# A two-layer transformer kernel: compressed values in one product of 79 rows, later steps of the compression chains, and an earlier transpose of x

## The chip, the cores and the metric

The kernel runs on one core of a Trainium2 chip. The time is device microseconds of one execution, from the first to the last thing that the core does. Three runs of the kernel before gave 2173.02, 2168.36 and 2178.68 us; the median is 2173.02. The profile is of a further execution, and its times are counted from the start of its span.

The engines are named as the profile names them: PE is TensorE (matmuls and transposes), PEld its weight loads, DVE is VectorE, ACT is ScalarE, POOL is GpSimd, and SP issues most DMA transfers.

## The reference

256 tokens of width 2048 go through two layers, all in float32. Layer 0 is an attention by stick breaking and a feed-forward part, layer 1 the native sparse attention (NSA) and a feed-forward part. The change touches the first products of layer 0 and the NSA. Of the NSA, cut to what matters:

```python
# 16 heads of 128 in 4 groups; n_cmp = (256 - 32) // 16 + 1 = 15 compressed blocks
def compress_blocks(x, pe, w1, w2):            # x: (B, G, T, 128)
    idx = arange(n_cmp)[:, None] * 16 + arange(32)[None, :]
    flat = (x[:, :, idx] + pe).reshape(B, G, n_cmp, 32 * 128)
    return gelu(flat @ w1) @ w2

kc_blk = rms_norm(compress_blocks(kc, pe[0], w1[0], w2[0]), k_norm_g[0])
vc_blk = compress_blocks(vc, pe[1], w1[1], w2[1])
p_cmp  = softmax(where(mask_c, q @ kc_blk.T * scale - slope * dist_c, NEG_INF)) * mask_c
o_cmp  = p_cmp @ vc_blk                        # 15 rows deep
o      = gates[0] * o_cmp + gates[1] * o_slc + gates[2] * o_win
```

With 256 tokens all four selection blocks are always taken, so selected and window attention are both dense causal attentions over 256 keys.

## The kernel before, in words

**Precision by split.** A float32 operand is split into a high part, rounded to the matmul's own format (F32R), and a low part, the remainder. ScalarE writes the high part (a Copy into an F32R tile) and VectorE the low part (a subtraction). Each product is then three matmuls: high by high, high by low, low by high. `split` (line 131) does it for weights, `split_evac` (line 313) for results in PSUM.

**Projections.** Weights come in raw tiles of 2 x 128 x 512 (five buffers, 512 KB each) and are split into `whi` and `wlo` tiles (four buffers each). `chunk_N` (line 153) and `chunk_T` (line 192) do the 12 or 24 matmuls of one such chunk. Between their high and their low part, and again behind them, they call `pump()`.

**Work beside the projections.** Attention, compression and the like are generators in the list `beside` (lines 101 to 121). Each `pump()` serves only the first in the list: it adds rate/2 to that generator's account and takes a step for each whole unit; a `yield 1` ends the pump's turn. `drain()` runs all that is left, to the end, without heeding what is yielded. `keys` is put at the front of the list with a waiting time of three, the others at the end; compression, gates and attention have the rate 1.8, keys the rate 2. Outside a part marked `manual_schedule` a planner then orders each engine's instructions, by their order in the program and by its own estimate of when operands and buffers are ready; within that part (the first stage, lines 511 to 576) the order is the written one.

**The first stage.** Queries and keys of the first head group are accumulated chunk by chunk while x arrives. `make_x` (line 325) takes two column blocks of x, transposes them on TensorE (line 330), and ScalarE and VectorE evacuate them as `xhi` and `xlo` (lines 335 and 337). In the loop at line 559 each pass does the queries' chunk, then `make_x` for the next pass, then the keys' chunk; in the first pass `make_x` stands behind the keys' chunk. The split of the next queries' weights (line 575) is written behind both.

**The NSA stage (lines 707 to 1053).** Projections of the compression inputs, then `compress(0)` and `compress(1)` (line 745) are spawned, the gates' projection follows, and then for each of four groups the keys and values, and the queries. `compress` adds the position part (8 steps), splits (4), multiplies by `w1` (16 steps, line 779), adds the halves (line 786), transposes (line 790), applies the gelu (lines 795 to 804) and multiplies by `w2`: for keys one product, a norm and a transpose (lines 814 to 830), for values four products into a PSUM tile of 15 rows (line 809) and a split into `vc`, high and low. At the first group `drain()` ends both compressions before the pool of the attention tiles is opened.

`attention` (line 937) does for each token tile t of 128: scores and exponentials of four heads (`scores`, line 865), then the division by the sums and the gates (`scale`, line 889), then `values` (line 903). In `values` each block of keys is transposed for four heads (line 925, into 8 or 15 rows for the compressed block, 128 for others), evacuated as high and low (`pT`), and multiplied in `product` by three matmuls of 512 columns (lines 917 to 919). The compressed block is the first of each.

Of the kernel before, what the change touches and what calls it, by code (L numbers as in the profile page):

```python
# [8 lines left out]
F32 = mybir.dt.float32  # L9
F32R = mybir.dt.float32r  # L10
# [5 lines left out]
P = 128  # L16
T = 256
NT = T // P
# [15 lines left out]
SW = 2 * P + CH  # L34
GATES = 3 * NH
# [4 lines left out]
def hybrid_kernel(  # L40
# [457 lines left out]
    with tc.tile_pool(name="sbp", bufs=2) as sp:  # L498
# [12 lines left out]
        with tc.manual_schedule(engines={mybir.EngineType.PE, mybir.EngineType.DVE, mybir.EngineType.Activation,  # L511
# [47 lines left out]
            for i in range(NX):  # L559
                if i + 1 < NX:  # L560
                    load_x(i + 1)
                    rq.append(load(sb_w_qkv[0], (i + 1) * KC, KC, 0, NB))
                    rk.append(load(sb_w_qkv[0], (i + 1) * KC, KC, D, NB))
                first, last = i == 0, i + 1 == NX
                if first:
                    pq = split_first(rq[0])
                pk = split(rk[i], (FAR, FAR))
                chunk_first(*pq) if first else chunk_T(psq0, pq, i * KC, 0, False, last)
                if not last and not first:
                    make_x((i + 1) * KC, G_SB)  # L570
                chunk_T(psk0, pk, i * KC, 0, first, last)
                if not last:
                    if first:
                        make_x(KC, G_SB)
                    pq = split(rq[i + 1], (FAR, FAR))
                ssq("sb", i, NX)
# [130 lines left out]
    with tc.tile_pool(name="nsa", bufs=2) as ap, ExitStack() as last:  # L707
# [7 lines left out]
        vc = ap.tile([P, 2, G, P], F32R, name="vc", bufs=1)  # L715
# [29 lines left out]
        def compress(i, cT):  # L745
# [42 lines left out]
            yield 1  # L788
            ph = bank(att, "att")
# [14 lines left out]
            nc.vector.tensor_tensor(a, a, b, op=OP.mult)  # L804
            yield
            pk = bank(att, "att")
            if i == 1:
                for g in range(G):
                    nc.tensor.matmul(pk[:NCMP, g * P:(g + 1) * P], a[:, g * NCMP:(g + 1) * NCMP], w2c[:, 1, :],
                                     start=True, stop=True)  # L810
                vcf = vc[:NCMP].rearrange("p i g d -> p i (g d)")
                split_evac(vcf[:, 0, :], vcf[:, 1, :], pk[:NCMP, :])
                return
# [7 lines left out]
            nc.vector.tensor_scalar(kc[:GC, :], pk[:GC, :P], r[:GC, :], None, op0=OP.mult)  # L821
            yield 1
# [42 lines left out]
        def scores(g, j, t, q, khi, klo, sums):  # L865
# [16 lines left out]
            pc = at.tile([P, na, CH], F32, tag=f"pc{t}", name="pc", bufs=HG + 1)  # L882
# [6 lines left out]
        def scale(g, t, pr, sums):  # L889

            nc.vector.reciprocal(sums, sums)
            gv = gates[:, t, :].rearrange("p (b h) -> p h b", b=3)[:, g * HG:(g + 1) * HG, :]
            nc.vector.tensor_tensor(sums, sums, gv, op=OP.mult)
            for s in range(3):
                for j in range(HG):
                    o = pr[j][s]
                    f = sums[:, j, s:s + 1]
                    if s == 2:
                        nc.scalar.activation(o, o, AF.Copy, scale=f)
                    else:  # L900
                        nc.vector.tensor_scalar(o, o, f, None, op0=OP.mult)

        def values(g, t, pr, v):

            nk = (CH, NCMP)[t]
            blocks = [(nk, lambda j: pr[j][0].rearrange("p a c -> p (a c)")[:, :nk], vc[:nk, :, g, :])]
# [7 lines left out]
            def product(last):  # L914
                nonlocal n
                lv, pT = late.pop(0)
                nc.tensor.matmul(po, lv[:, 0, :], pT[:, 0, :], start=n == 0, stop=False)  # L917
# [4 lines left out]
            for w, src, lv in blocks:  # L922
# [4 lines left out]
                split_evac(pT[:w, 0, :], pT[:w, 1, :], ptp[:w, :])  # L927
# [100 lines left out]
        for g in range(G):  # L1028
# [19 lines left out]
            if g == 0:  # L1048
                first.close()
                at = last.enter_context(tc.tile_pool(name="att", bufs=2))  # L1050
            hq = [heads(ps[t].rearrange("p (h d) -> p h d", h=HG), t, HG) for t in range(NT)]
# [41 lines left out]
```

## Time and profile before

| what | value |
|---|---|
| times of three runs | 2168.36, 2173.02 and 2178.68 us |
| the profiled execution: span | 2160.6 us (a time of its own is not recorded beside it) |
| median of the runs over that span | 12.4 us |
| TensorE busy | 2150.9 us, 14914 matmuls |
| VectorE, ScalarE, GpSimd busy | 1595.6, 1207.8 and 42.5 us |
| read from memory | 401.83 MB, 187 GB/s over the span |

The span runs from the first to the last instruction; the time of a run also has what lies around it. Matmuls are pipelined, so their durations overlap. What a matmul costs is the distance from its start to the start of the next. In a row of the timeline there stand the start, the time from that start to the end of the last of so many instructions, the engine, the line, the operation, what is written and what is read, the shapes, the count and, in brackets, how long the engine had been idle and what it had waited for.

### The profile page before, as it was taken

What the parts mean: (1) busy time and instruction counts of PE and PEld (TensorE: products, weight loads), DVE (VectorE), ACT (ScalarE), POOL (GpSimd) and SP (SyncE); (2) the same over time, 40 slices, a digit from 0 to 9 for tenths busy, and PEclk for the clock granted to TensorE, in tenths of its full rate; (3) what the DMA queues carried; (4) which work ended last, traced back from release to release, by engine and by line L of the source; (5) the groups of instructions that cost most, each with busy time, mean ns of one, the idle gap of its engine ahead of it and who ended that gap; (6) DMA issues with size and microseconds to landing.
All of it is one profiled execution on the core that took longest, in us unless ns stands there. A gap on an engine that the chain in (4) does not pass through costs nothing.

```text
span 2160.6 us, 37393 instructions
## 1 busy us (share of the span) xinstructions
PE 2150.9 (100%) x14914; PEld 1983.8 (92%) x14914; DVE 1595.6 (74%) x2238; ACT 1207.8 (56%) x1639; POOL 42.5 (2%) x75
## 2 busy tenths in 40 slices
PE   9999999999999999999999999999999999999999
PEld 8999988998998999999898888889989989989998
DVE  5656556568878878878777877756778788788786
ACT  5555565555555555555546666655555555555553
POOL 0000000000000000000000011000000000000000
PEclk9999999999999999999999999999999999999999
DMA  7655555665665665665667554446656656656664
GB/s 232 208 176 173 159 176 176 186 198 190 206 195 185 205 195 189 223 195 186 206 179 222 166 142 133 145 159 186 202 192 190 205 177 217 200 188 205 196 200 161
DMA packets 260790, 406.35 MB, mean 188 GB/s; under 512 B 13188, under 2 KB 91912, under 8 KB 260616
## 3 DMA queue, kind: packets, MB, share of 16 engines
q1 hardware_dynamic: 259800, 403.52, 59.8%
q8 instruction: 116, 1.90, 0.4%
q10 hardware_dynamic: 816, 0.46, 0.1%
q14 instruction: 58, 0.48, 0.1%
HBM read 401.83 MB, written 2.10 MB: 187 GB/s over the span
## 4 chain that ended last, share of the span: by engine, by line
PE 99%; DVE 0%; DMA 0%; POOL 0%; ACT 0%; issue 0%; SPq 0%; DVEq 0%; ACTq 0%
PE acc L206 42%; PE acc L157 37%; PE att L273 13%; PE att L157 1%; PE att L925 1%; PE att L330 1%; PE att L917 0%; PE att L918 0%; PE att L919 0%; PE att L612 0%; PE att L660 0%; PE att L871 0%; PE att L873 0%; PE att L872 0%; PE att L849 0%; DMA raw<-in_sb_w_qkv_dram 0%
## 5 line engine op out<-in xcount | busy, mean ns | idle before, releaser
L135 ACT ACTIVATE hi<-raw 128x1024 fp32r<-128x1024 f32 x591 | 625.5, 1060 | 522.5 <-PE acc L206 217.9
L137 DVE TENSOR_TENSOR lo<-raw,hi 128x1024 fp32r<-128x1024 f32 x591 | 719.5, 1221 | 252.7 <-ACT hi L135 232.7
L206 PE MATMUL acc<-xs,hi 128*128 128x256 f32 x5360 | 669.1, 277 | 1.9 <-ACT hi L135 1.9
L206 PEld LDWEIGHTS acc<-xs,hi 128*128 128x128 f32 x5360 | 638.7, 188 | 3.1 <-ACT hi L135 2.1
L206 PE MATMUL acc<-xs,lo 128*128 128x256 f32 x2680 | 359.6, 277 | 0.0
L206 PEld LDWEIGHTS acc<-xs,lo 128*128 128x128 f32 x2680 | 329.5, 188 | 0.0
L157 PE MATMUL acc<-hi,yhi 128*128 128x512 f32 x828 | 324.6, 392 | 0.0
L157 PE MATMUL acc<-hi,ylo 128*128 128x512 f32 x828 | 322.9, 390 | 0.0
L157 PE MATMUL acc<-lo,yhi 128*128 128x512 f32 x828 | 223.0, 391 | 0.0
L135 ACT ACTIVATE hi<-ts 128x1024 fp32r<-128x1024 f32 x112 | 118.9, 1061 | 169.7 <-DVE ts L253 87.0
L157 PEld LDWEIGHTS acc<-lo,yhi 128*128 128x128 f32 x828 | 154.6, 188 | 32.0 <-issue 0.4
L157 PEld LDWEIGHTS acc<-hi,yhi 128*128 128x128 f32 x828 | 155.5, 188 | 29.7 <-ACT yhi L316 0.2
L157 PEld LDWEIGHTS acc<-hi,ylo 128*128 128x128 f32 x828 | 155.5, 188 | 29.6 <-DVE ylo L317 0.2
L157 PE MATMUL acc<-hi,xs 128*128 128x512 f32 x704 | 177.1, 392 | 0.0
L246 DVE TENSOR_TENSOR ts<-raw 128x512 f32<-128x512 f32 x112 | 77.0, 691 | 118.2 <-DMA raw<-in_mlp_w_dram 118.0
L157 PEld LDWEIGHTS acc<-hi,xs 128*128 128x128 f32 x704 | 130.3, 188 | 26.6
L137 DVE TENSOR_TENSOR lo<-ts,hi 128x1024 fp32r<-128x1024 f32 x112 | 136.5, 1219 | 9.6 <-ACT hi L135 9.3
L251 ACT ACTIVATE shi<-raw 128x768 fp32r<-128x768 f32 x112 | 94.6, 845 | 60.4 <-PE att L273 41.1
L254 DVE TENSOR_TENSOR slo<-raw,shi 128x768 fp32r<-128x768 f32 x112 | 106.5, 951 | 0.5 <-PE att L273 0.5
L157 PE MATMUL acc<-lo,xs 128*128 128x512 f32 x352 | 97.5, 397 | 0.0
L273 PE MATMUL att<-hi,ss 128*128 128x256 f32 x672 | 95.9, 279 | 0.0
L273 PEld LDWEIGHTS att<-hi,ss 128*128 128x128 f32 x672 | 86.4, 189 | 0.0
(250 smaller groups left out, 2247.4 us busy)
## 6 DMA issues: line engine op xcount, KB each, us to landing
raw<-in_mlp_w_dram SPq DMA_DIRECT2D x512, 512.0 KB, 4.3
raw<-in_sb_w_qkv_dram SPq DMA_DIRECT2D x95, 512.0 KB, 3.9
raw<-in_nsa_w_in_dram SPq DMA_DIRECT2D x50, 512.0 KB, 3.7
raw<-in_sb_w_out_dram SPq DMA_DIRECT2D x32, 512.0 KB, 4.0
raw<-in_nsa_w_in_dram SPq DMA_DIRECT2D x64, 256.0 KB, 3.3
raw<-in_nsa_w_out_dram SPq DMA_DIRECT2D x32, 512.0 KB, 3.6
w1t<-in_nsa_cmp_w_dram SPq DMA_DIRECT2D x8, 512.0 KB, 4.8
h<-in_x_dram SPq DMA_DIRECT2D x8, 256.0 KB, 4.5
```

What stands on the lines that cost most here:

```text
L135: nc.scalar.activation(hi, raw, AF.Copy)
L137: nc.vector.tensor_tensor(lo, raw, hi.bitcast(F32), op=OP.subtract)
L157: mm = lambda a, b, k, t, s, e: nc.tensor.matmul(ps[t], a[:, k, t * P:(t + 1) * P], b, start=s, stop=e)
L206: nc.tensor.matmul(o, w, x[:, k0 + kk, :], start=s, stop=e, skip_group_check=True)
L246: nc.vector.tensor_tensor(ts[:, :2, :], flat[:, W:3 * W].rearrange("p (a n) -> p a n", a=2), b12, op=OP.subtract)
L251: nc.scalar.activation(hi, flat[:, :3 * W], AF.Copy)
L254: nc.vector.tensor_tensor(lo, flat[:, :3 * W], hi.bitcast(F32), op=OP.subtract)
L273: nc.tensor.matmul(ps[i], a, w, start=s, stop=e, skip_group_check=True)
L330: nc.tensor.transpose(ps[:, j * T + t * P:j * T + (t + 1) * P], h[:, t, (kp + j) * P:(kp + j + 1) * P], ident)
L925: nc.tensor.transpose(ptp[:w, j * P:(j + 1) * P], src(j), ident)
```

## The change

It has three parts.

1. In the first pass of the first stage `make_x` for the second pass is written ahead of the keys' chunk, as in all other passes.
2. The compressed values are multiplied in one matmul in place of three. The gated weights of the compressed keys are written three times side by side, at columns 0, 32 and 64 of a tile that was zeroed once (`pcs`), by the scaling itself. Their transpose has 79 rows. Rows 0 to 63 are rounded to the high part, and rows 64 to 78 are turned into the low part. The values' product with `w2` is widened in the same way (`a3`) to 79 rows: rows 0 to 14 and 64 to 78 high, rows 32 to 46 low. One matmul over these rows then adds high by high, high by low and low by high.
3. In `compress` there are two more yields, one ahead of the first transpose and one ahead of the transpose of the keys, and the yield behind the gelu becomes a `yield 1`.

The tiles of the unscaled compressed weights now have one tag for both token tiles, with five buffers in all.

```diff
+ST = 32
+SK = 2 * ST + NCMP
...
-                if not last and not first:
+                if not last:
                     make_x((i + 1) * KC, G_SB)
                 chunk_T(psk0, pk, i * KC, 0, first, last)
                 if not last:
-                    if first:
-                        make_x(KC, G_SB)
                     pq = split(rq[i + 1], (FAR, FAR))
...
-        vc = ap.tile([P, 2, G, P], F32R, name="vc", bufs=1)
+        vc = ap.tile([P, G, P], F32R, name="vc", bufs=1)
...
             yield 1
             yield 1
+            yield 1
             ph = bank(att, "att")
             nc.tensor.transpose(ph[:, :2 * GC], hs[:2 * GC, 0, :], ident[:2 * GC, :2 * GC])
...
-            nc.vector.tensor_tensor(a, a, b, op=OP.mult)
-            yield
+            if i == 1:
+                a3 = cp.tile([P, G, 3 * ST], F32, name="a3", bufs=1)
+                nc.vector.memset(a3, 0.0)
+                av, bv = [
+                    u.rearrange("p (g n) -> p g n", g=G).unsqueeze(2).to_broadcast([P, G, 3, NCMP]) for u in (a, b)
+                ]
+                nc.vector.tensor_tensor(
+                    a3.rearrange("p g (s n) -> p g s n", s=3)[:, :, :, :NCMP], av, bv, op=OP.mult
+                )
+            else:
+                nc.vector.tensor_tensor(a, a, b, op=OP.mult)
+            yield 1
             pk = bank(att, "att")
             if i == 1:
                 for g in range(G):
-                    nc.tensor.matmul(pk[:NCMP, g * P:(g + 1) * P], a[:, g * NCMP:(g + 1) * NCMP], w2c[:, 1, :],
-                                     start=True, stop=True)
-                vcf = vc[:NCMP].rearrange("p i g d -> p i (g d)")
-                split_evac(vcf[:, 0, :], vcf[:, 1, :], pk[:NCMP, :])
+                    nc.tensor.matmul(pk[:SK, g * P:(g + 1) * P], a3[:, g, :SK], w2c[:, 1, :], start=True, stop=True)
+                vcf = vc.rearrange("p g d -> p (g d)")
+                nc.scalar.activation(vcf[:SK, :], pk[:SK, :], AF.Copy)
+                mid = slice(ST, 2 * ST)
+                nc.vector.tensor_tensor(vcf[mid, :], pk[mid, :], vcf[mid, :].bitcast(F32), op=OP.subtract)
                 return
...
             yield 1
             yield 1
+            yield 1
             pt = bank(att, "att")
...
-            pc = at.tile([P, na, CH], F32, tag=f"pc{t}", name="pc", bufs=HG + 1)
+            pc = at.tile([P, na, CH], F32, tag="pc", name="pc", bufs=HG + 1)
...
-                    if s == 2:
+                    if s == 0:
+                        n = (t + 1) * CH
+                        w = pcs[t][:, j, :].rearrange("p (s n) -> p s n", s=3)[:, :, :n]
+                        src = o.rearrange("p a c -> p (a c)").unsqueeze(1).to_broadcast([P, 3, n])
+                        nc.vector.tensor_scalar(w, src, f, None, op0=OP.mult)
+                    elif s == 2:
...
-            nk = (CH, NCMP)[t]
-            blocks = [(nk, lambda j: pr[j][0].rearrange("p a c -> p (a c)")[:, :nk], vc[:nk, :, g, :])]
+            blocks = [(SK, lambda j: pcs[t][:, j, :SK], vc[:SK, g, :])]
...
-                nc.tensor.matmul(po, lv[:, 0, :], pT[:, 0, :], start=n == 0, stop=False)
+                if n == 0:
+                    nc.tensor.matmul(po, lv, pT[:, 0, :], start=True, stop=False)
+                    n += 1
+                    return
+                nc.tensor.matmul(po, lv[:, 0, :], pT[:, 0, :], start=False, stop=False)
...
-                split_evac(pT[:w, 0, :], pT[:w, 1, :], ptp[:w, :])
+                if w == SK:
+                    nc.scalar.activation(pT[:w, 0, :], ptp[:w, :], AF.Copy)
+                    low = slice(2 * ST, w)
+                    nc.vector.tensor_tensor(
+                        pT[low, 0, :], ptp[low, :], pT[low, 0, :].bitcast(F32), op=OP.subtract
+                    )
+                else:
+                    split_evac(pT[:w, 0, :], pT[:w, 1, :], ptp[:w, :])
...
                 at = last.enter_context(tc.tile_pool(name="att", bufs=2))
+                pcs = [at.tile([P, HG, 3 * ST], F32, name=f"pcs{t}", bufs=1) for t in range(NT)]
+                for t in range(NT):
+                    nc.vector.memset(pcs[t], 0.0)
```

## The prediction

> **What bounds the kernel now.** I read the page first, then a table of stretches, then the list of TensorE's own waits. From the page, the span, the busy time of TensorE and the chain that ended last:
>
> ```profile
> span 2160.6 us, 37393 instructions
> ...
> PE 2150.9 (100%) x14914; PEld 1983.8 (92%) x14914; DVE 1595.6 (74%) x2238; ACT 1207.8 (56%) x1639; POOL 42.5 (2%) x75
> ...
> PE 99%; DVE 0%; DMA 0%; POOL 0%; ACT 0%; issue 0%; SPq 0%; DVEq 0%; ACTq 0%
> ```
>
> The table by stretches has the length, then busy time (and count) of PE, PEld, DVE, ACT and POOL, then the granted clock, the DMA share and GB/s:
>
> ```profile
> 20.00:400.00 380.00, 380.00 (x2491) 346.15 (x2490) 217.37 (x256) 220.05 (x310) 14.04 (x34) 1.00 0.59 181
> ...
> 1160.00:1200.00 40.00, 38.57 (x194) 30.81 (x193) 29.93 (x61) 22.24 (x37) 4.06 (x4) 1.00 0.73 210
> 1200.00:1220.00 20.00, 20.00 (x110) 16.64 (x109) 18.64 (x56) 17.44 (x63) 0.81 (x2) 1.00 0.38 106
> 1220.00:1420.00 200.00, 200.00 (x988) 162.47 (x987) 149.53 (x317) 128.34 (x299) 17.75 (x12) 1.00 0.48 140
> ```
>
> TensorE is never idle from 20 to 400 us nor in the sparse attention after 1200 us, and the clock is 1.00 throughout. So a matmul taken away anywhere shortens the end by its own pitch, and a TensorE wait taken away shortens it by that wait, as long as no other engine takes over. There is little of the second kind: of all waits of TensorE (total us, times, longest) this is the longest, and two more that the change can touch stand in part 3.
>
> ```profile
> PE acc L206 <- ACT hi L135: 1.9, 1, 1.9
> ```
>
> **Part 1, x's second tiles ahead of the first keys.** This wait is at 15.33 us, in front of the second chunk of queries. The waits of the DMA-issuing queue, its timeline and that of the other engines, and last what the trace says of the 512 KB of weights of this second chunk:
>
> ```profile
> SPq L94 <- DMA h<-in_x_dram: 0.5, 1, 0.5
> ```
>
> ```profile
> 9.42 0.24 SPq L94 DMA_DIRECT2D grows<-in_nsa_k_norm_g_dram  x1
> 9.79 1.23 DVE L137 TENSOR_TENSOR lo<-raw,hi 128x1024 fp32r<-128x1024 f32 x1 [1.58 <-ACT hi L135]
> 10.03 2.05 PE L206 MATMUL acc<-xs,hi 128*128 128x256 f32 x16
> 12.86 0.60 PE L330 MATMUL att<-ident,h 128*128 128x128 f32 x4
> 13.49 0.84 ACT L335 ACTIVATE xs<-att,gT 128x256 fp32r<-128x256 f32 x2 [3.74 <-PE att L330]
> 14.22 1.05 ACT L135 ACTIVATE hi<-raw 128x1024 fp32r<-128x1024 f32 x1
> 15.33 2.08 PE L206 MATMUL acc<-xs,hi 128*128 128x256 f32 x16 [1.87 <-ACT hi L135]
> ```
>
> ```profile
> L142 SPq DMA_DIRECT2D raw<-in_sb_w_qkv_dram x1: 469/469/469, 3.3 to 3.3; - x1
> ...
> DMA to landing us min/median/max: 7.5/7.5/7.5
> ```
>
> ScalarE stands idle for 3.74 us until the transposes (L330), which TensorE reaches only behind the whole keys chunk, and the split of the second queries stands behind ScalarE's evacuation of them in its order. The new order sends the four transposes first. They need x's second piece. Its landing has no record; but the small load L94 had waited for a transfer into h and went out at 9.42, so I put the landing at 9.4 us, before the 10.03 at which TensorE is free. Step by step: transposes at 10.03, evacuation 0.63 later (13.49 − 12.86) at 10.66, two pieces until 11.50, split of the weights (landed at 3.25 + 7.5 = 10.8) until 12.55. TensorE meanwhile pays 0.35 for the transposes (a pitch measured in part 2) and does the keys until 12.86 + 0.35 = 13.2, when hi is ready. The keys' lo is ready at 9.79 + 1.23 = 11.0. So the second queries start at 13.2 in place of 15.33: **−2.1 us**. That is also the most there is, since TensorE has no other wait there. At the other bound it is 0: with a piece of x that landed at 12.1 us the same chain (landing, then 0.63 + 0.84 + 1.05 plus the keys behind the transposes) would end where it ends now. The SP queue issues the same transfers in the same order, and VectorE and ScalarE keep their order too; only TensorE's changes. Next in line is the ring of five raw tiles, whose loads wait for VectorE's splits; these come earlier as well.
>
> **Part 2, one product of 79 rows.** TensorE's timeline in the first group, second token tile: the four transposes of the compressed weights with their successor, the three products with their successor, then the same for an ordinary block:
>
> ```profile
> 1231.42 0.60 PE L925 MATMUL att<-ident,pc 128*15 128x128 f32 x4
> 1231.77 1.17 PE L157 MATMUL acc<-lo,xs 128*128 128x512 f32 x4
> ...
> 1235.13 0.50 PE L917 MATMUL att<-pT,vc 15*128 15x512 f32 x1
> 1235.47 0.39 PE L918 MATMUL att<-pT,vc 15*128 15x512 f32 x1
> 1235.70 0.38 PE L919 MATMUL att<-pT,vc 15*128 15x512 f32 x1
> 1236.02 1.19 PE L157 MATMUL acc<-lo,xs 128*128 128x512 f32 x4
> 1237.05 0.60 PE L925 MATMUL att<-ident,p 128*128 128x128 f32 x4
> 1237.40 0.48 PE L917 MATMUL att<-pT,v 128*128 128x512 f32 x1
> 1237.72 0.39 PE L918 MATMUL att<-pT,v 128*128 128x512 f32 x1
> ```
>
> Durations overlap, so I count from start to start. The block of three takes 1236.02 − 1235.13 = 0.89 us: 0.34 for the first, 0.23 for the second, 0.32 for the third, before a product of other rows. One product stays. At best it costs the 0.32 that the first product of an ordinary block costs behind its transposes; at worst the entry of 0.34 and the 0.09 that the third pays over the second, 0.43. There are 8 such blocks (4 groups, 2 token tiles): 8 x 0.57 = 4.6 or 8 x 0.46 = 3.7. 79 rows lie between 15 and 128, so I take the middle, **−4.2 us**.
>
> What the block adds: its transposes have 79 columns in place of 8 or 15. Four of them take 0.35 us to the successor with 15 columns and 0.35 with 128, so nothing on the path. Their weight loads are longer, however (from the view of line 925):
>
> ```profile
> L925 PEld LDWEIGHTS att<-ident,p x96: 137/140/144, 1213.0 to 1412.8; 128*128 128x128 f32 x96
> ...
> L925 PEld LDWEIGHTS att<-ident,pc x32: 83/88/96, 1210.8 to 1402.9; 128*8 128x8 f32 x16, 128*15 128x15 f32 x16
> ```
>
> Were they in the open, 32 x (140 − 88) ns = 1.7 us would come back. The Trainium skill, "TensorE: Matmul & The Clock Gate", section "LDWEIGHTS (loading the stationary operand)", has a load cost its columns divided by 1.2 ns; 71 or 64 columns more would be, as an estimate, 32 times 53 to 59 ns, 1.8 us, and the sum below 5.0 instead of 6.8. The rows agree that the load grows and show that its growth is hidden.
>
> VectorE and ScalarE, from the views of lines 316 and 901 and the timeline of the start:
>
> ```profile
> L316 ACT ACTIVATE pT<-att x32: 569/577/602, 1212.2 to 1413.2; 128x512 fp32r<-128x512 f32 x24, 8x512 fp32r<-8x512 f32 x4, 15x512 fp32r<-15x512 f32 x4
> ```
>
> ```profile
> L901 DVE TENSOR_SCALAR pc<-pc,sums x32: 224/226/234, 1210.3 to 1402.6; 128x8 f32<-128x8 f32 x16, 128x16 f32<-128x16 f32 x16
> L901 DVE TENSOR_SCALAR p<-p,sums x32: 278/315/353, 1210.8 to 1403.5; 128x128 f32<-128x128 f32 x16, 128x256 f32<-128x256 f32 x16
> ```
>
> ```profile
> 4.76 0.17 DVE L90 MEMSET grows<- 128x128 f32 x1
> ```
>
> The evacuations keep their count; 8, 15 or 128 rows make 569 to 602 ns, so 79 rows cost the same. Scaling into three copies writes 24 or 48 elements for 8 or 16: between 226 and 278 ns, at most 32 x 0.05 = 1.7 us of VectorE over four groups. Three memsets (a3, two pcs) of 128x384 are at most three times 0.17 each, 1.5 us, once. The fullest stretch is 1200 to 1220, where VectorE has 20.00 − 18.64 = 1.36 us free; two memsets and the eight wider scalings of one group would bring at most 1.0 + 0.4 = 1.4. I cost it at **0**, since the weight splits run ahead. From the waits between 1080 and 1420 us:
>
> ```profile
> ACT hi L135 <- PE acc L157: 59.2, 45, 3.0
> ```
>
> Forty-five times ScalarE stood until TensorE gave a buffer back, so a split late by a microsecond is not missed. Without that cover it costs the 1.4. The compressed weights now have five tiles for both token tiles together instead of five each; a fifth exp must find the first scaling done.
>
> **Part 3, the chains wait half a chunk longer.** TensorE's timeline again:
>
> ```profile
> 1167.09 0.43 PE L814 MATMUL att<-w2c,ga 128*60 128x128 f32 x2
> ...
> 1171.17 0.24 PE L825 MATMUL att<-ident,kc 60*128 60x60 f32 x1 [0.46 <-DVE kc L821]
> ...
> 1180.32 3.95 PE L779 MATMUL att<-ws,bs 128*120 128x256 f32 x32
> ...
> 1187.49 0.32 PE L790 MATMUL att<-ident,hs 120*128 120x120 f32 x1 [0.94 <-DVE hs L786]
> ```
>
> I count the chain's steps on paper: 0.9 of a step per pump, two pumps per chunk, only the first generator in the list served, and the keys' generator in front for six pumps. The first chain's last step (L825) falls on pump 9 of the first group's queries, the middle of their fifth chunk, and with two more yields on pump 12, three half chunks later. From L814 to L825 there are then four half chunks instead of two. The 0.46 goes. It has a price: one step that slips past the end of the keys-and-values projection is the gelu's, and the keys' generator now stands in front of it. It is written on pump 7, and L814 on pump 8, one half chunk behind it instead of seven. The gelu's VectorE steps in the trace, first and last:
>
> ```profile
> 1156.01 0.21 DVE L795 COPY ga<-att 128x60 f32<-128x60 f32 x1
> ...
> 1162.26 0.21 DVE L804 TENSOR_TENSOR ga<-ga,gb 128x60 f32<-128x60 f32 x1
> ```
>
> They took 6.5 us, between splits. L790 comes half a chunk later now, so they can run from about 1157.4 to 1163.9, and L814 comes at about 1168.4: I cost this at 0, as long as VectorE fills its gaps with them before their turn, as it has to. If they begin only behind the splits of their turn, L814 waits. The second chain gets 6 steps before drain() now, and 3 then; drain() runs the rest without heeding any yield, which the 32 products in one piece at 1180.32 show. So its wait of 0.94 at L790 isn't touched by the new yields. The yield after the gelu changes nothing: at 0.9 per pump no pump holds two steps. **−0.5 us**; bounds −1.4 if both waits go, since the planner orders the code anew, and +0.9 if L814 gets a wait like that of L790. Behind a TensorE instruction that waits stand all later matmuls of the projection.
>
> **The sum**: 2.1 + 4.2 + 0.5 = 6.8 us off the span of 2160.6, 2153.8. The median of the runs, 2173.02, lies 12.4 us above that span; with as much around it, 2166.2.
>
> **Rivals.**
> (a) *x is late.* For it: the landing is inferred, and DMA is at its busiest there. Against: even at 12.1 us nothing is lost. Part 1 gives 0: 2168.3.
> (b) *VectorE becomes the bound between 1200 and 1220 us.* For: 93% busy. Against: the 59.2 us above. The two blocks saved there (1.05) are lost and 1.4 paid: 2168.7.
> (c) *The transposes' longer weight loads are in the open.* For: the 52 ns. Against: the equal pitch. 1.7 back: 2167.9. (By the skill's rule named above, 1.8 back.)
> (d) *Slower.* The planner writes a new order for the stage, with TensorE's instructions behind VectorE's results that come later than it reckons, as at L790, where the price was 0.94. In the first attention group VectorE hands over about 12 times (two compression steps, four score tiles, four products, two transposes). If each waited 0.94: 11.3 − 6.8 = 4.5 above, 2177.5. It decides from the eighth such wait on (6.8 / 0.94 = 7.2). Against: between 1200 and 1420 TensorE had no wait at all.
>
> **How the numbers follow.** Forecast 0.60, (a) 0.15, (b) 0.12, (c) 0.05, (d) 0.08. The runs before lie between 2168.36 and 2178.68, −4.7 to +5.7 around their median, which is about as large as the whole effect. The range begins at 2166.2 less 1.3 (part 2 at 4.6, part 3 at 1.4) and less that spread, about 2159, and goes to (b) plus the spread, about 2175; (d) and the tails are left out. What a measurement here can tell from no change is about 0.5%, 10.9 us. The forecast needs another 4 us to count as faster: 0.09. Slower takes more than (d) gives: 0.05. Within 0.5%: 0.86.
>
> **What would show it.** In the changed profile: the second queries at about 13.2 us with no TensorE wait; one product of 79 rows about 0.32 to 0.43 us ahead of its successor; four 79-column transposes at 0.35; no wait at L825 nor L814, that of L790 still there; no new wait between 1200 and 1420; a span near 2154. A wait of the first queries for x, a TensorE wait in the first group, or a span that is not at least 3 us shorter would make the prediction wrong.

## The result, and the profile after

The changed kernel takes 2157.83 us (median of 6 runs, 2154.16 to 2161.9), the kernel before beside it 2173.32 (6 runs, 2168.36 to 2178.68). The ratio is 0.992, with a 95% interval of 0.9902 to 0.9939. The prediction was 2166.2 with a range of 2159 to 2175, so the gain was about twice as large as forecast. The prediction had given 0.86 to a change within 0.5%; the ratio is 0.8% under 1.

The span fell from 2160.6 to 2152.4 us, by 8.2, where the sum was 6.8. From the page of the changed kernel, span, busy time and the chain that ended last:

```profile
span 2152.4 us, 37355 instructions
...
PE 2145.5 (100%) x14898; PEld 1983.1 (92%) x14898; DVE 1597.2 (74%) x2241; ACT 1205.3 (56%) x1639; POOL 42.6 (2%) x75
...
PE 99%; DVE 0%; POOL 0%; ACT 0%; issue 0%; DVEq 0%; ACTq 0%; POOLq 0%
```

TensorE still sets the end. Its matmuls are 16 fewer, as they should be (8 blocks, two each). The list of all its waits, in full, and the stretches that answer to those shown of before (length, busy time of PE, PEld, DVE, ACT and POOL, granted clock, DMA share, GB/s):

```profile
PE att L520 <- POOL ident masks.py:199: 1.6, 1, 1.6
PE att L791 <- DVE hs L786: 0.9, 1, 0.9
PE acc L539 <- ACT hi L532: 0.4, 1, 0.4
```

```profile
20.00:400.00 380.00, 380.00 (x2491) 346.16 (x2490) 217.00 (x255) 219.60 (x307) 14.11 (x34) 1.00 0.59 182
1198.00:1218.00 20.00, 20.00 (x112) 17.22 (x111) 18.78 (x55) 17.24 (x63) 1.73 (x3) 1.00 0.28 80
1218.00:1418.00 200.00, 200.00 (x999) 164.92 (x998) 154.84 (x322) 131.93 (x306) 16.68 (x11) 1.00 0.50 148
```

The waits ahead of the second queries (1.9 us) and of the keys' transpose (0.5) are gone, that ahead of the second chain's transpose (0.9) is still there, and no other has come. VectorE is as full in the first attention group as before (18.78 of 20 us), and TensorE does not wait for it.

**The start.** The timeline of the changed kernel, x's transposes and both chunks of queries and keys around them:

```profile
10.14 0.60 PE L332 MATMUL att<-ident,h 128*128 128x128 f32 x4
10.49 2.07 PE L208 MATMUL acc<-xs,hi 128*128 128x256 f32 x16
10.78 0.84 ACT L337 ACTIVATE xs<-att,gT 128x256 fp32r<-128x256 f32 x2 [0.77 <-PE att L332]
11.51 1.06 ACT L137 ACTIVATE hi<-raw 128x1024 fp32r<-128x1024 f32 x1
...
13.31 1.98 PE L208 MATMUL acc<-xs,hi 128*128 128x256 f32 x16
```

Each row stands within 0.15 us of the step that the prediction wrote for it, and the second queries start at 13.31 without a wait, where 13.2 was forecast.

**The product.** The timeline in the first group, second token tile: the four wide transposes with their successor, and the one product with its successor; then from the views of the two lines the weight loads and the scaling:

```profile
1228.01 0.60 PE L946 MATMUL att<-ident,pcs 128*79 128x128 f32 x4
1228.36 1.17 PE L159 MATMUL acc<-lo,xs 128*128 128x512 f32 x4
...
1231.56 0.47 PE L935 MATMUL att<-pT,vc 79*128 79x512 f32 x1
1231.87 1.09 PE L159 MATMUL acc<-lo,xs 128*128 128x512 f32 x4
```

```profile
L946 PEld LDWEIGHTS att<-ident,pcs x32: 145/147/151, 1209.2 to 1395.1; 128*79 128x79 f32 x32
```

```profile
L915 DVE TENSOR_SCALAR pcs<-pc,sums x32: 219/231/244, 1208.8 to 1394.8; 128x24 f32<-128x24 f32 x16, 128x48 f32<-128x48 f32 x16
```

The product is 0.31 us ahead of its successor here (the block of three was 0.89), the transposes 0.35. Their weight loads rose from 88 to 147 ns and cost nothing on the path. Three copies are scaled in 231 ns where one took 226.

**The chains.** The first chain's product and transpose, and the second chain's transpose:

```profile
1165.87 0.43 PE L826 MATMUL att<-w2c,ga 128*60 128x128 f32 x2
...
1171.91 0.27 PE L838 MATMUL att<-ident,kc 60*128 60x60 f32 x1
...
1184.87 0.32 PE L791 MATMUL att<-ident,hs 120*128 120x120 f32 x1 [0.95 <-DVE hs L786]
```

**Where the span went.** I cut each profiled execution at three marks: the first squaring of the first feed-forward part, the first product of the gates, and the first squaring of the second feed-forward part. Lengths in us:

```
                 to the first  feed-forward  sparse     second feed-
                 squaring      part          attention  forward part
before           419.3         708.3         368.7      664.3
changed          417.1         708.3         362.5      664.5
```

The start brought 2.1 (419.26 − 417.14 before rounding) and the sparse attention 6.2. In these two executions the feed-forward parts are equal. Yet the medians differ by 15.5 us, not by 8.2. A run's time and the span of the same execution are both recorded for the changed kernel: 2154.16 and 2152.4, so 1.8 us lie around a span. The profiled execution of the kernel before therefore took about 2162.4, well under the lowest of its six runs. That profile showed a quiet execution, not a typical one.

### The profile page after: what moved, and what is told of

It reads as the page before. It is cut to its first block, busy times and chain, and to the rows that moved or that the text cites. A ratio compares the mean times of both kernels' runs of the same rounds, so it can differ in the third digit from the quotient of the medians.

```text
span 2152.4 us, 37355 instructions
## 1 busy us (share of the span) xinstructions
PE 2145.5 (100%) x14898; PEld 1983.1 (92%) x14898; DVE 1597.2 (74%) x2241; ACT 1205.3 (56%) x1639; POOL 42.6 (2%) x75
## 4 chain that ended last, share of the span: by engine, by line
PE 99%; DVE 0%; POOL 0%; ACT 0%; issue 0%; DVEq 0%; ACTq 0%; POOLq 0%
PE acc L208 43%; PE acc L159 37%; PE att L275 13%; PE att L159 1%; PE att L332 1%; PE att L946 1%; PE att L612 0%; PE att L660 0%; PE att L884 0%; PE att L940 0%; PE att L886 0%; PE att L885 0%; PE att L939 0%; PE att L938 0%; PE att L862 0%; PE att L779 0%
```

## One part at a time

The first experiment does each of the three parts alone and, as a measure, the kernel before once more, all on one chip.

In only_product stands part 2 of the change with all that belongs to it (`a3`, `pcs`, `vc`, `values` and `product`); only_x is the kernel before with

```diff
-                if not last and not first:
+                if not last:
                     make_x((i + 1) * KC, G_SB)
                 chunk_T(psk0, pk, i * KC, 0, first, last)
                 if not last:
-                    if first:
-                        make_x(KC, G_SB)
```

and only_waits the kernel before with

```diff
+            yield 1
             ph = bank(att, "att")
...
-            yield
+            yield 1
             pk = bank(att, "att")
...
+            yield 1
             pt = bank(att, "att")
```

> The kernel before, with nothing changed, against itself. What is open: the spans differ by 8.2 us (2160.6 to 2152.4), the medians by 15.5. Theory 1 (a few us come and go from execution to execution, in work that the change does not touch, and the profiled execution of before was a quick one): no difference beyond some 4 us, and a profile of it that is a few us longer than 2160.6 with the excess in a stage that the change does not touch. Theory 2 (the old order of the first stage is sensitive to when the data arrive): a longer profile has its excess in the first 30 us.

> The kernel before with only x's second tiles transposed ahead of the first keys. Theory 1 (each part is worth the TensorE time that it frees): 2.1 us less in the first stage and nothing after it; 0 to 5 us in the medians. Theory 2 (this part also takes away a wait that only slower executions have): 8 us or more less in the medians.

> The kernel before with only the compressed values in one product of 79 rows. Theory 1: 4.2 us less (3.7 to 4.6), all of it between 1200 and 1410 us, medians 2 to 7 us less. Rival, that freed TensorE time is worth more than itself because VectorE or ScalarE get on sooner too: 7 us or more.

> The kernel before with only the compression chains waiting longer. Theory 1: the wait of 0.46 us at the transpose of the compressed keys goes, that of 0.94 at the second chain's first transpose stays; 0.5 us less, not to be told from none in the medians. Rival, that the new order of the stage which the planner writes is what moves the time: a difference of several us either way, and no TensorE wait to explain it.

Measured beside 2171.1 us for the kernel before (34 runs, 2162.62 to 2179.27): before_again 2171.3 (ratio 1.0, 0.9987 to 1.0014), only_x 2170.47 (0.9992, 0.9979 to 1.0005), only_product 2158.11 (0.9952, 0.9936 to 0.9967), only_waits 2171.06 (0.9995, 0.9981 to 1.0009). The product alone brings nearly the whole gain, and the other two nothing that can be told. Its 13.0 us are far more than the 2 to 7 that theory 1 gave the medians. By the marks:

```
                 to the first  feed-forward  sparse     second feed-
                 squaring      part          attention  forward part
before_again     420.7         711.0         368.9      669.6
only_x           418.7         713.6         368.8      669.4
only_waits       419.0         708.4         368.3      674.6
only_product     419.4         709.3         362.9      664.3
```

The parts do what they should where they stand: the waits take 0.5 off the sparse attention, the product 5.9. The mark of the start mixes other things in, for the first keys begin at 12.07 us in only_x and at 9.7 to 10.2 in the other three. So x's tiles are read from their own stretch, from the first keys (or from x's transposes, where these stand ahead of them) to the second queries: 3.19 us in only_x, 5.30 to 5.32 in the others.

But the second feed-forward part, which no edit touches, takes 5 to 10 us longer in the three kernels without the new product, as theory 1 of before_again had it. The first one took longer as well in two of them (711.0 and 713.6 against 708.3). The waits of TensorE in before_again and in only_waits show most of it; of the 5.5 us in the first line 4.0 lie in the second feed-forward part, of the 6.3 in the other line all:

```profile
PE att L273 <- DVE slo L254: 5.5, 6, 2.0
```

```profile
PE att L273 <- DVE slo L254: 6.3, 3, 3.5
```

Line 273 holds the matmuls of the seven-product chunks of the feed-forward parts, and `slo` is the low part of their weights. The longest of these waits in only_waits, by the timeline (SP's issue of the two next weight tiles, TensorE before the wait, VectorE, TensorE behind it):

```profile
2112.25 1.50 SPq L142 DMA_DIRECT2D raw<-in_mlp_w_dram  x2
...
2117.44 0.28 PE L273 MATMUL att<-hi,ylo 128*128 128x256 f32 x1
2117.55 0.69 DVE L246 TENSOR_TENSOR ts<-raw 128x512 f32<-128x512 f32 x1 [3.06 <-DMA raw<-in_mlp_w_dram]
2120.22 0.95 DVE L254 TENSOR_TENSOR slo<-raw,shi 128x768 fp32r<-128x768 f32 x1
2121.22 0.79 PE L273 MATMUL att<-slo,yhi 128*128 128x256 f32 x2 [3.51 <-DVE slo L254]
2121.82 0.41 PE L273 MATMUL att<-slo,ss 128*128 128x256 f32 x1
```

VectorE waited 3.06 us for weights in flight, `slo` was finished at 2121.17, and TensorE stood for 3.51. All eleven waits for `slo` of over 0.4 us that the traces have in the second feed-forward part, with the old product or the new, end 3.5 to 3.7 us after VectorE took up a weight tile that it had waited for. Ten of the eleven lie at two places, 261 to 276 or 617 to 626 us behind the part's first squaring. Two traces with the new product wait at the second place too, but for 0.43 and 0.47 us.

In the trace shown, TensorE was slow for a while behind the wait as well: the second row below has a granted clock of 0.89, so 0.11 x 15 = 1.65 us are lost.

```profile
2100.00:2115.00 15.00, 15.00 (x88) 13.24 (x87) 12.83 (x16) 9.61 (x11) 0.00 (x0) 1.00 0.67 217
2115.00:2130.00 15.00, 11.49 (x59) 9.96 (x58) 9.55 (x13) 4.07 (x5) 0.00 (x0) 0.89 0.44 154
```

The mean clock of an execution shows without a profile that the clock was at half for a time, though not where: 3.4 us at half take 0.0008 off it, whether they lie here, at the start (last section) or at the end of the span, where TensorE has finished. Of the 34 runs of the kernel before on this chip 24 have 0.997 to 0.999, nine of them 0.998 or less; of the 11 of only_product two, 2158.11 with 0.999 and its slowest, 2170.03, with 0.998.

## Is it the size of the program or the places of its instructions?

The changed kernel has 36 fewer TensorE instructions ahead of the second feed-forward part. Instructions are fetched by transfers of their own (queue q8 of the page of before: 116 packets, 1.90 MB), so their number may move the fetches against the weights. Three kernels shift them. changed_16_more_first has sixteen more transposes at the start, changed_16_more_last sixteen behind the last matmul, and before_16_fewer_first sixteen fewer at the start. In this order:

```diff
-            keep_warm(12)
+            keep_warm(20)
...
-            keep_warm(6)
+            keep_warm(14)
```

```diff
+        tail = bank(att, "att")
+        for _ in range(16):
+            nc.tensor.transpose(tail[:, :P], h[:, 1, D - P:], ident)
```

```diff
-            keep_warm(12)
+            keep_warm(2)
...
-            keep_warm(6)
```

> The changed kernel, with nothing altered, as the mark for the two below. All theories: a median 12 to 16 us below that of the kernel before, granted clock 1.000 in most executions.

> The changed kernel with 16 more of the idle transposes that keep TensorE warm at the start, 8 in each of the two places: TensorE's instruction stream is then again as long ahead of both feed-forward parts as in the kernel before (21138 to 21142 instructions at the second part's first product of the seven-product kind, 21106 in the changed kernel). They cost up to 1.8 us at the start. Theory I (the 16 matmuls less move the places at which TensorE's instructions are fetched, 16 KB at a time over the same 16 DMA engines, away from weights that arrive with less than a microsecond to spare): the stalls of the feed-forward parts come back, the median is 7 to 10 us above that of the changed kernel and the clock below 1.000 in most executions. Rival P (the cause lies in the sparse attention's stage or in the banks of PSUM that the second feed-forward part gets, 6 and 7 exchanged): 0 to 2 us above the changed kernel, clock 1.000.

> The changed kernel with 16 idle transposes behind everything else, beside the last transfers out. The program is as long as that of the kernel before, but nothing moves ahead of them. Theory I: as the changed kernel, 0 to 2 us above it. Rival S (the size of the program, and with it where things lie in memory, is what counts): 7 us or more above it.

> The kernel before without 16 of its 18 idle transposes at the start (10 of the first 12 and all of the 6 behind them): TensorE's instruction stream is then as long ahead of the second feed-forward part as in the changed kernel (21111 instructions instead of 21142), everything else as before. A colder start may cost up to 2 us. Theory I: 5 to 8 us faster than the kernel before, clock 1.000 in most executions. Rival P or S: 0 to 2 us slower than before, clock below 1.000 in most.

Beside 2167.15 us for the kernel before (18 runs): changed_again 2155.32 (ratio 0.9936, 0.9918 to 0.9955), changed_16_more_first 2157.49 (0.9949, 0.993 to 0.9969), changed_16_more_last 2154.25 (0.9935, 0.9917 to 0.9953), before_16_fewer_first 2167.08 (0.9996, 0.9983 to 1.001). The second feed-forward part took 664.3, 664.2 and 664.3 us in the three and 673.2 in the last. The 11.8 us of changed_again are just short of the 12 to 16 that were expected. Neither sixteen more nor sixteen fewer instructions moved a kernel to the other side, so theory I failed in both. The size of the program is excluded; the places of the fetches are not the cause in the simple form tried.

## Is it the banks, or the time freed?

Through the second feed-forward part both kernels run the same instructions in the same order on every engine. By the order in which tiles are handed out, what differs is that two PSUM banks, 6 and 7, are exchanged; the traces name no bank and do not show this. Eight transposes ahead of it, using seven tiles of which the fourth is released late, are meant to exchange them back, in each kernel. Two more kernels separate the product's time from its form: the kernel before with two of its three products left out, and the changed kernel with two products more.

Ahead of the second call of `mlp`, in before_banks_exchanged and changed_banks_exchanged:

```diff
+        turn = []
+        for i in (0, 1, 2, 3, 4, 5, 3, 6):
+            if i == len(turn):
+                turn.append(bank(att, "att"))
+            nc.tensor.transpose(turn[i][:, :P], ident, ident)
```

In `product`, in before_two_left_out and then in changed_two_put_back:

```diff
+                if n == 0:
+                    n += 1
+                    return
                 nc.tensor.matmul(po, lv[:, 1, :], pT[:, 0, :], start=False, stop=False)
```

```diff
-                    nc.tensor.matmul(po, lv, pT[:, 0, :], start=True, stop=False)
+                    for i in range(3):
+                        nc.tensor.matmul(po, lv, pT[:, 0, :], start=True, stop=i < 2)
```

> The kernel before, with eight transposes (0.7 us) ahead of the second feed-forward part that use seven PSUM tiles in such an order that banks 6 and 7 are exchanged in all that follows, as they are in the changed kernel. Instructions and their order are otherwise those of before. Theory B (the banks decide whether the seven-product chunks of the second feed-forward part wait for their weights): that part takes 664 to 666 us with no TensorE wait at its low sums over 0.5 us, nearly all executions have a mean clock of 1.000, and the median is 5 to 7 us under that of the kernel before. Theory T (what decides is the TensorE time freed in the sparse attention) and theory N (another piece of the new product): 669 to 676 us in most executions, clocks of 0.997 to 0.999 as before, median 0 to 2 us over that of the kernel before.

> The changed kernel with the same eight transposes, by which its second feed-forward part gets the banks that the kernel before has there. Theory B: that part takes 669 to 676 us, TensorE waits 3 us or more at its low sums, clocks of 0.997 to 0.999 in most executions, and the median is 7 to 10 us under that of the kernel before instead of 12 to 15. Theories T and N: 664 to 666 us, clocks of 1.000, median 11 to 15 us under that of the kernel before.

> The kernel before with two of the three products of the compressed block left out (the output lacks the compressed values' high-by-low and low-by-high parts); tiles, banks and evacuations stay as they are. What goes is by the rows of before 0.23 + 0.32 us in each of 8 blocks, 4.4 us. Theory T: the second feed-forward part takes 664 to 665 us, clocks of 1.000, and the median is 10 to 13 us under that of the kernel before. Theories B and N: it still takes 669 to 676 us in most executions with clocks of 0.997 to 0.999, and the median is 4 to 5 us under that of the kernel before. The sparse attention's share alone tells besides whether it falls by 4.4 us or by the 6.0 that the 79-row product brought.

> The changed kernel with its 79-row product done three times in a row for each block, of which the last is the one that counts: 16 matmuls of 512 columns are put back, 8 x 2 x 0.23 = 3.7 us or, with the clean pitch of a first product, up to 5. Tiles, banks and evacuations are those of the changed kernel. Theory T: the second feed-forward part waits for its weights again, 669 to 676 us and clocks of 0.997 to 0.999, median 3 to 5 us under that of the kernel before. Theories B and N: 664 to 665 us, clocks of 1.000, median 8 to 11 us under that of the kernel before, that is 4 to 5 over the changed kernel.

Beside 2167.63 us for the kernel before (30 runs, 2163.02 to 2177.49): before_banks_exchanged 2166.41 (ratio 0.9998, 0.9981 to 1.0014), changed_banks_exchanged 2157.43 (0.9958, 0.9942 to 0.9974), before_two_left_out 2162.82 (0.9973, 0.9959 to 0.9986), changed_two_put_back 2158.62 (0.9973, 0.9957 to 0.9989).

```
                         to the first  feed-forward  sparse     second feed-
                         squaring      part          attention  forward part
before_banks_exchanged   421.0         709.0         369.4      665.3
changed_banks_exchanged  417.1         708.3         363.3      664.3
before_two_left_out      422.7         708.3         365.1      665.5
changed_two_put_back     417.3         708.3         365.4      665.0
```

If the transposes do exchange them, the banks are not it: with those of before the changed kernel stays at 664.3, and with those of the changed kernel the kernel before is no faster (its one profile, 665.3, is a quick one, but its twelve runs reach 2179.34). Theory T asked for a median 10 to 13 us lower in before_two_left_out, and it was 4.8 lower. In changed_two_put_back the median is 9.0 lower than the kernel before, which theories B and N forecast, but three of its twelve runs, to 2174.21, have clocks of 0.999; freed time alone does not decide it. That it has a share is suggested by the spreads: the runs of before_two_left_out lie within 6.3 us, where those of the kernel before beside it lie within 14.5, and those of changed_two_put_back lie within 17.2. With eleven and twelve runs this is a hint and not shown.

The sparse attention tells more. Start-to-start distances of TensorE summed by kind (us, from the traces):

```
                              before  before_two_  only_     changed
                                      left_out     product
compressed product             7.14    3.38         2.27      2.27
its transposes (32)            3.16    3.16         2.85      2.86
the other transposes (96)      9.20    9.20         8.65      8.65
projections (1152)           269.86  269.95       269.53    269.06
whole stage                  368.69  365.07       362.92    362.46
```

Leaving two products out gives 3.8 us; the 79-row product gives 4.9, as one product of 79 rows costs 2.27 / 8 = 0.28 us and one of 8 or 15 rows 3.38 / 8 = 0.42. A further 0.9 comes from the transposes, 0.3 from the compressed block's own and 0.6 from the others.

## Which part of the program holds the rest?

Twins without the second feed-forward part (the residual is written out instead, so that part of the computation is missing), and the changed kernel with part 1 undone:

```diff
-        mlp(1, "m1", mp, done1, ov)
+        drain()
+        nc.sync.dma_start(ov, h)
```

```diff
-                if not last:
+                if not last and not first:
                     make_x((i + 1) * KC, G_SB)
                 chunk_T(psk0, pk, i * KC, 0, first, last)
                 if not last:
+                    if first:
+                        make_x(KC, G_SB)
```

> The kernel before without the second feed-forward part: the residual stream is written out behind the sparse attention (the output lacks that part). To be read against its changed twin on the same chip, not against the whole kernel. Theory F (of the 12 to 15 us between the medians, what the profiles of quiet executions do not account for arises in the second feed-forward part): the two twins' medians differ by 8 to 10 us, that is the 8.2 of the quiet profiles (2160.6 less 2152.4) and at most 1.7 for a half-rate clock window at the start, and both spread alike. Theory E (the rest arises in the parts ahead of it): they differ by 11 us or more, and the kernel before spreads wider.

> The changed kernel without the second feed-forward part, the twin of the one above (the output lacks that part as well). Theory F: its median lies 8 to 10 us under its twin's. Theory E: 11 us or more.

> The changed kernel with the transposes of x's second tiles put back behind the first keys. Theory H (the wait of 1.9 us ahead of the second queries costs its own length, and in some executions a TensorE clock granted at half for one window, 1.7 us more): the median is 2 to 4 us above the changed kernel's on the same chip, part of the executions has a mean clock of 0.999, and a profile of such a one has a granted clock under 1 in its first 20 us. Rival: 2.0 us, all clocks 1.000.

> The changed kernel as it is, on the same chip as the three others, as their measure: 12 to 15 us under the kernel before, clocks of 1.000, second feed-forward part 664 to 665 us.

The twins take 1482.72 us (4 runs, 1482.53 to 1483.39) and 1474.01 (4 runs, 1473.63 to 1475.76): 8.7 apart, as theory F has it. The spread of the kernel before, 2162.82 to 2175.46 in the same minutes, shrinks to 0.9 us in the four runs (2.1 in those of its twin). So on this chip its spread arises in the second feed-forward part, and what lies ahead of it differs by 8.7 us. The whole kernels differ by 2166.95 − 2155.55 = 11.4 on that chip, where 12 to 15 were expected (changed_third: ratio 0.9947, 0.9926 to 0.9968); 11.4 − 8.7 = 2.7 us of the medians would be the second feed-forward part. In the quickest runs that part is equal: 2162.82 − 1482.53 = 680.3 and 2153.99 − 1473.63 = 680.4. The interval of that ratio is 6.9 to 16.0 us, so on this chip the 2.7 is not clear of noise; in the first result (0.9902 to 0.9939, 13.3 to 21.3 us) the excess over 8.7 is. The chips differ too: the median of the kernel before is 2171.1 on that of only_product and 2166.95 to 2167.63 on the other two.

changed_x_late takes 2157.95 us (6 runs; ratio 0.9951, 0.9934 to 0.9968), 2.4 over changed_third, and 419.0 against 417.0 to the first squaring. Half of its runs have a clock of 0.999, as theory H has it; its profiled run has 1.00 throughout, and the four profiles at half clock in the last section show what the wait does to the clock.

## Why the prediction was wrong

Step by step:

- **Part 1 was right**: 2.1 forecast; the stretch from the first keys (or x's transposes ahead of them) to the second queries took 5.23 to 5.32 us in the nine profiles with the old order and 3.17 to 3.27 in the nine with the new. The mark of the start alone would not show it: changed_again, without that wait, has 419.1 us, as its first keys begin at 12.04 us. What the forecast left out is the clock, below, worth 1.7 us in four of the nine profiles that have the wait.
- **Part 2 was mis-sized**: 4.2 forecast with a best case of 4.6, and 5.9 measured (368.8 in only_x less 362.9 in only_product). The 0.89 of the old block was right (7.14 / 8). "At best it costs the 0.32" was not: it costs 0.28. And the transposes, costed as "nothing on the path", gave 0.9 back. The prediction read those of one token tile, 0.35; over all eight blocks the compressed block's took 3.16 / 8 = 0.40 before and 0.36 after. Why the other blocks' became 0.6 shorter was not followed up.
- **Part 3 was right**: 0.46 of 0.5 came (362.92 − 362.46), at the wait that was named; the wait at the second chain stayed, at 0.95.
- **Rivals**: (a), x late, fell with the start at 13.31; (b) and (c) with a TensorE that never waits after 1198 us and transposes at 0.35; (d) with the list of waits. The Trainium skill's rule named with (c) ("TensorE: Matmul & The Clock Gate", section "LDWEIGHTS (loading the stationary operand)") made 53 to 59 ns of the added columns; the growth here, 147 − 88 = 59, agrees and is hidden. The loads themselves do not follow that rule: 79 columns, 66 ns by it as an estimate, took 147, more than the 140 of 128 columns.
- **The step that failed** is the last of the sum, "with as much around it". The 12.4 us between the span and the median of before do not lie around the span; 1.8 do. The other 10.6 were the distance of a quiet execution from a typical one, and that distance did not stay: in the changed kernel its counterpart is 2157.83 − 2154.16 = 3.7. From 2153.8 with 1.8 around and that 3.7 the same sum gives 2159.3; the 1.5 left to the 2157.83 measured is about the 1.7 that part 2 brought beyond its 4.2. No rival had a stage that the change does not touch getting steadier, although the three runs of before, 10 us apart with a quiet profile under all of them, asked where that spread arises.
- **The range**: 2166.2 less 1.3 and less the 4.7 by which a run lay under the median is 2160.2; the 2159 comes from the 5.7 above it.

**What stays open.** Shown is that the kernel before loses time in the second feed-forward part, where weights land late, in four of six profiles with the old product (669.4 to 674.6 us) and in none of eight with the new one (664.2 to 665.4), that every long wait for `slo` there stands behind such a late tile, and that the program's size does not make the difference. The PSUM banks do not either, if the transposes exchanged them. Why the weights come in time behind the new product is not settled. Whether less freed time, other instruction places on VectorE and ScalarE, the chip or plain chance between few profiles has a part in it was not separated: the twelve runs of changed_two_put_back lie between both kinds.

## What to carry to other kernels

Before a sum is set against a median, compare the profiled execution's span with the fastest and the typical run: if it is quicker than all of them, the median holds stalls that this profile does not show, and they may go or stay whatever the edit does where it stands. Leaving the last stage out of both kernels is a short way to find which stage spreads. One deep product in place of three shallow ones saved more than the two products: the remaining one cost 0.28 us instead of 0.42.

## What the hardware did that was not expected

A TensorE wait of 1.87 us can halve the clock behind it. The timeline and the stretches of one us in before_again, at the wait that part 1 removes:

```profile
15.18 3.68 PE L206 MATMUL acc<-xs,hi 128*128 128x256 f32 x16 [1.87 <-ACT hi L135]
```

```profile
14.00:15.00 1.00, 0.00 (x0) 0.00 (x0) 0.79 (x2) 1.00 (x2) 0.00 (x0) 1.00 0.94 327
15.00:16.00 1.00, 0.82 (x4) 0.83 (x5) 0.93 (x2) 1.00 (x6) 0.00 (x0) 0.64 0.88 335
16.00:17.00 1.00, 1.00 (x7) 1.00 (x7) 0.49 (x2) 0.86 (x1) 0.00 (x0) 0.50 0.36 123
17.00:18.00 1.00, 1.00 (x6) 1.00 (x6) 1.00 (x1) 0.00 (x0) 0.00 (x0) 0.50 0.40 51
18.00:19.00 1.00, 1.00 (x8) 1.00 (x7) 0.12 (x1) 0.00 (x0) 0.00 (x0) 0.65 0.90 324
```

Sixteen matmuls that took 2.08 us in the quiet profile take 3.68. The clock is short by 0.36 + 0.5 + 0.5 + 0.35 = 1.71 us, so it stood at half for 3.4 us. This happened in four of the nine profiled executions that have the wait. The traces' clock records change on a grid of 3.413 us. The place of the wait, counted in such windows from the trace's first clock record, and the largest share of one window in which TensorE was idle tell the cases apart:

```
kernel                  wait from .. to    idle share   next window
before_16_fewer_first   1.39 .. 1.93       0.549        half
before_two_left_out     1.28 .. 1.82       0.549        half
before_banks_exchanged  2.33 .. 2.88       0.549        half
before_again            2.42 .. 2.97       0.549        half
changed_x_late          2.45 .. 3.00       0.548        full
before_no_second_ffn    1.96 .. 2.51       0.509        full
only_waits              2.53 .. 3.08       0.468        full
before                  2.65 .. 3.20       0.349        full
only_product            2.68 .. 3.23       0.323        full
```

Where the wait lies within one window, the next runs at half; where the grid cuts it in two, it does not. So such a wait costs its 1.87 us and, by the luck of the phase, 1.7 more. The same share sorts the windows of all eighteen traces, 10944 of them: behind each of the 20 with 0.549 or more idle the clock is at half, behind all with 0.548 or less it is full, but for one that was itself at half (before_16_fewer_first, at 1934.8 us). A single wait of 1.60 us inside one window (only_x, at 1040.57 us, share 0.470) left the clock alone, and one of 2.50 us (only_waits, at 1758.99 us, share 0.731) did not, although it reached just past its window's end. Between 0.51 and 0.55 only changed_x_late lies, on the border.

The Trainium skill, "TensorE: Matmul & The Clock Gate", section "What's actually happening", has the clock fall after an idle window of about 3.4 us; the window's length agrees, but here 1.87 us of idleness within it, 55%, was enough.
